# Seven half-size products for the down projection, earlier operand transfers for the SSD output product, and later squares in the attention norm

## The chip, the cores and the metric

The kernel runs on one core of a Trainium2 chip. A core has five engines with a queue each: TensorE (PE, with its weight loads shown as PEld), VectorE (DVE), ScalarE (ACT), GpSimd (POOL) and SyncE (SP), which here only issues transfers. The metric is the device time of one execution in microseconds; three runs are given and the median is compared.

## The reference

One decoder block over x (1024 tokens by 1024 channels, float32). What the change touches is, cut to the core:

```python
y = ssd_branch(...)                                # 1024 x 1024
merged = gate_ssd * (y_ssd @ w_ssd_o) + gate_att * (y_att @ w_attn_o)
o = rms_norm(o, subln_w, eps=SUBLN_EPS) * (1.0 - lam_init)   # per head of the differential attention
u = causal_dwconv(h2 @ w_up, conv_ffn_w, conv_ffn_b)         # 1024 x 5632
u_gate, u_val = jnp.split(u, 2, axis=-1)
f = (jax.nn.gelu(u_gate, approximate=True) * u_val) @ w_down # (1024 x 2816) @ (2816 x 1024)
x = x + g2 * rms_norm(f, post_norm2_w)
```

## The kernel before

All large products are float32 made of three passes: each operand is split into a high part `hi` (rounded to float32r) and a low part `lo = raw - hi`, and three matmuls add hi·hi, hi·lo and lo·hi into one PSUM bank. `split` (L80 to L82) makes the parts: ACT writes `hi` (L81), DVE writes `lo` (L82) from the raw tile and `hi`. Weights arrive by SP transfers into `wraw` (3 buffers) and are split into `whi` and `wlo` (4 buffers each). A matmul has a 128x128 stationary operand and a moving operand of up to 512 columns. Tiles that live longer come from 43 slots of 4 KB per partition (`Slots`), handed out in the order in which they were given back; a slot's new owner waits for the old one's last reader.

The stages in order of time are: the first norm and adaLN (0 to about 62 us of the span); the SSD's input product `xbc` with its convolution (L393 to L422), beside which DVE sums the rows of the adaLN weights (`ada_sum`, L364 to L370); the `z` product (L441 to L457); the chunked SSD scan; gates; q and k; the SSD output product `so` (L820 to L835); the differential attention (L851 to L1113); the attention output product `ao` (L1127 on); `w_out`, the second norm; the up projection `up` (L1294 to L1330); and the down projection, whose banks are called `fx` and `fy` (L1336 to L1390).

**Order of work.** A scheduler orders each engine's instructions before the run, by its own estimates of their durations and by when operands and buffers come free. Regions under `manual_schedule` keep the written order for the engines named: PE in `xbc`; PE, DVE and ACT in the attention. Nothing of `so`, `up` or `down` is written out by hand. An engine runs its queue in order; a waiting instruction holds all behind it. SP's queue issues every transfer of the kernel.

**`so`, L820 to L835.** For each of 8 blocks j: load the weight block (`load_block`), load the gate `gth` from DRAM (one buffer), 48 matmuls into a two-bank tile, two DVE instructions (L830) that multiply by the gate into `mout` (one buffer), store `mout` to `msd`. For j = 2 and 3 the first heads' q and k are loaded too.

**Attention.** Items (j, i) are head pair j and query block i. For each item: scores (PE), mask and maximum (DVE, L976 and L977 or L986 and L987), exponentials with row sums (ACT, L989, L997, L1000), reciprocal and combination into `p` (DVE, L1003 to L1005), transposes of `p` (PE, L1013), copies `aT` (ACT, L1014), product with v (PE, L1026). Between these, dense matmuls of later blocks are filled in (`fill`). After four items `norm_o` (L1030 to L1048) copies the four output blocks, and returns `squares` (four ACT instructions that square and sum, L1041); the next item's first turn runs them behind its scores and transposes and ahead of its exponentials. `first` and `second` (DVE, POOL and DVE again, L1035 to L1045) are background work behind.

**Up, L1294 to L1330.** The product h2 @ w_up is done by a scheme of seven half-size products in place of eight (with 2x2 blocks of both operands and sums of blocks, Strassen in Winograd's form). Per block pair `fb` (22 of them: gate block `fb`, value block `22 + fb`) there are 7 products of 12 matmuls each of 512 columns. `hl_tile` gives the split weights: 4 slots and the 8 `whi`/`wlo` buffers, 12 in turn. Bank `X` collects four products, `Y` two and `Z` one; between them ACT (L1305, L1313, L1315, L1321) and DVE (L1306, L1317, L1319) read the banks. Then the convolution (ACT L1325, DVE L1327), GELU (L1328), the gate product (DVE L1329) and the store of `g_` to DRAM (L1330).

**Down, L1336 to L1390.** For each half of the tokens the 22 blocks of `g_` are loaded (`gst`, 2 buffers of two blocks) and split into 22 slots; for each half of the channels 11 pairs of weight blocks are loaded and split, and 22 x 4 x 3 matmuls are added into 4 banks. That is 4 rounds of 264 matmuls. Each round ends with a sum of squares (ACT L1381) and a product (DVE L1382); the second round of a half also with the norm (DVE, POOL) and the store.

Of the kernel before, what the change touches and what calls it, by code (L numbers as in the profile page):

```python
# [17 lines left out]
P = 128  # L18
# [16 lines left out]
class Slots:  # L35
# [18 lines left out]
def kernel(ctx: ExitStack, tc: tile.TileContext, a: dict, out: bass.AP, dbg=None):  # L54
# [275 lines left out]
    gd = [dp.tile([P, S], F32, tag=f"gd{i}", name=f"gd{i}") for i in range(NFF)]  # L330
# [55 lines left out]
    brow = SL.get("brow")  # L386
    n_ada, rows_done = 0, 0
# [4 lines left out]
    with tc.manual_schedule(engines={EN.PE}):  # L392
        for b in range(12):  # L393
# [17 lines left out]
            xbcT.append(o)  # L411
            if b >= 2:
# [27 lines left out]
    n_ev = 0  # L440
# [17 lines left out]
    SL.put(*ev)  # L458
# [361 lines left out]
    gth = SL.get("gth")  # L820
    mout = SL.get("mout")
    for j in range(8):
        w = load_block(a["w_ssd_o"][j], f"wso{j}")
        ps = ps_mm(f"so{j}")
        SP.dma_start(gth, gsd[j])
        for half in range(2):
            block_half(ps[:, half, :], w, yT, half)
        for half in range(2):
            hsl = slice(half * HALF, (half + 1) * HALF)
            V.scalar_tensor_tensor(mout[:, hsl], gth[:, hsl], 1.0, ps[:, half, :], op0=ALU.add, op1=ALU.mult)  # L830
        SP.dma_start(msd[j], mout)
        if j in (2, 3):
            s = j - 2
            load_qk(s, qst[0][s], kst[0][s], klo[0][s])
    SL.put(gth, mout)  # L835
# [194 lines left out]
    def norm_o(j, grp):  # L1030
# [16 lines left out]
        bg.extendleft([(("norm", j, grp), second), (None, lambda: None), (None, lambda: None), (None, first)])  # L1047
        return squares  # L1048
# [14 lines left out]
    with tc.manual_schedule(engines={mybir.EngineType.PE, mybir.EngineType.DVE, mybir.EngineType.Activation}):  # L1063
# [5 lines left out]
        pend = squares = None  # L1069
        for t, (j, i) in enumerate(items):  # L1070
# [6 lines left out]
            def first_turn():  # L1077
                x[0] = transposes(t, 0)
                if squares is not None:
                    squares()  # L1080
# [5 lines left out]
            squares = None  # L1086
# [18 lines left out]
            if i % 4 == 3:  # L1105
                squares = norm_o(j, i // 4)
                pend = (j, i // 4)
            elif i % 4 == 2:
                pend = None
        squares()  # L1110
# [109 lines left out]
    hls = [SL.get(f"hls{i}") for i in range(4)]  # L1220
# [4 lines left out]
    def hl_tile(name):  # L1225
        nonlocal n_hl
        i = n_hl % 12
        n_hl += 1
        if i < 4:
# [27 lines left out]
    for fb in range(2):  # L1257
# [36 lines left out]
    for fb in range(NFF):  # L1294
        cg, cv = cgv[fb % 2]
        e1, e2 = evs[fb % 2][:, 0, :], evs[fb % 2][:, 1, :]
        if fb >= 2:
# [24 lines left out]
        g_ = ug[fb % 2]  # L1322
# [7 lines left out]
        SP.dma_start(gd[fb], g_)  # L1330
    SL.put(*sab, *hls, *cgv[0], *cgv[1], *evs)
    for n, _ in order:
        SL.put(*HB[n])
    SL.put(*ug, uv)

    g2r = SL.get("g2r")  # L1336
    SP.dma_start(g2r, rowd[3].broadcast_to([P, D]))
    fo = [SL.get(f"fo{i}") for i in range(4)]
    x1r = [SL.get(f"x1r{i}") for i in range(4)]
    tf = SL.get("tf", F32, (P, HALF))  # L1340
    gst = [SL.get(f"gst{i}", F32, (P, 2, HALF)) for i in range(2)]
    gT = None
    ssf = const("ssf", [P, 8, 2])
    rsf = const("rsf", [P, 8])
    for half in range(2):
        if half == 1:
            SL.put(*gT)
        gT = [None] * NFF
        for fb in range(NFF):
            gT[fb] = new_hl(f"g{half}_{fb}")  # L1350
            st = gst[fb // 2 % 2][:, fb % 2, :]
            SP.dma_start(st, gd[fb][:, half * HALF : (half + 1) * HALF])
            split(gT[fb][:, 0, :], gT[fb][:, 1, :], st)
        for ch in range(2):
            if ch == 0:
                acs = [ps_wa(f"fx{half}_0"), ps_wa(f"fx{half}_1"), ps_wb(f"fx{half}_2"), ps_wc(f"fx{half}_3")]
            else:
                mmx = [ps_mm(f"fy{half}_{i}") for i in range(2)]
                acs = [mmx[i // 2][:, i % 2, :] for i in range(4)]
            last = half == 1 and ch == 1  # L1360
            wd = {}
            sched = []
            for kp in range(NFF // 2):
                if not last or kp < NFF // 2 - 3:
                    sched += [(kp, q) for q in range(4)]
            if last:
                sched += [(kp, q) for q in range(4) for kp in range(NFF // 2 - 3, NFF // 2)]
            for kp, q in sched:
                if kp not in wd:
                    wd[kp] = load_moving(a["w_down"], 2 * kp, 2, ch * HALF, HALF, f"wd{half}_{ch}_{kp}")  # L1370
                tsl = slice(q * P, (q + 1) * P)
                for kk in range(2):
                    k = 2 * kp + kk
                    wh, wl = wd[kp][0][:, kk, :], wd[kp][1][:, kk, :]
                    T.matmul(acs[q], gT[k][:, 0, tsl], wh, start=(k == 0), stop=False)  # L1375
                    T.matmul(acs[q], gT[k][:, 0, tsl], wl, start=False, stop=False)  # L1376
                    T.matmul(acs[q], gT[k][:, 1, tsl], wh, start=False, stop=(k == NFF - 1))  # L1377
            csl = slice(ch * HALF, (ch + 1) * HALF)
            for q in range(4):
                i = 4 * half + q  # L1380
# [75 lines left out]
```

## Time and profile before

| | us |
|---|---|
| median of 3 runs (lowest, highest) | 1979.33 (1977.42, 1981.37) |
| profiled execution, whole | 1979.32 |
| its span, first to last instruction | 1977.5 |
| mean granted TensorE clock | 0.992 |

The views below give busy time by engine; a group's row has the line, the engine, the operation, output <- inputs and the shapes, then busy us and mean ns of one, then the engine's idle time just ahead of them and what ended it. Matmuls overlap, so the mean of one is longer than the distance between two. The stage times above are read from such windows.

### The profile page before, as it was taken

Reading aid. Unit: us, or ns where it says so; the run is one execution under the profiler, and the core shown is the slowest. Engines: PE = TensorE matmul, PEld = TensorE weight load, DVE = VectorE, ACT = ScalarE, POOL = GpSimd, SP = SyncE. Lnnn points to the kernel's source line nnn. Section 1 sums busy time; section 2 is a strip of 40 time slices with the busy share of each in tenths; the row PEclk is TensorE's granted clock in tenths of the full one; section 3 lists DMA queues with packets and bytes.
Section 4 is the critical chain, followed back from the end, with each engine's and each line's share of the span. In section 5 each row is a group of like instructions: output and inputs, shape, how many; then the busy total and the mean of one; then the engine's idle time right before and its main releaser. Section 6 shows DMA issues by size and latency. Waiting matters only on the chain.

```text
span 1977.5 us, 24442 instructions
## 1 busy us (share of the span) xinstructions
PE 1905.0 (96%) x9260; PEld 1579.5 (80%) x9260; DVE 1167.4 (59%) x1782; ACT 834.7 (42%) x1606; POOL 117.0 (6%) x114
## 2 busy tenths in 40 slices
PE   6999999999999999999999999979999999999997
PEld 4787998878888788888887887758888888788886
DVE  6967334565172247767666445599787777664322
ACT  5532225554232135655556322366454554543221
POOL 0000002542010000000000000000000000000000
PEclk9999999999999999999999999989999999999999
DMA  9834232235337636565623552212222222574531
GB/s 303 297 117 161 78 108 79 91 107 177 117 75 226 220 106 177 154 168 147 183 89 136 182 185 107 93 50 100 96 75 86 84 77 86 175 245 144 181 97 63
DMA packets 120414, 269.06 MB, mean 136 GB/s; under 512 B 13284, under 2 KB 44644, under 8 KB 120296
## 3 DMA queue, kind: packets, MB, share of 16 engines
q1 hardware_dynamic: 120296, 267.50, 42.5%
q8 instruction: 73, 1.20, 0.2%
q14 instruction: 45, 0.37, 0.1%
HBM read 201.37 MB, written 66.08 MB: 135 GB/s over the span
## 4 chain that ended last, share of the span: by engine, by line
PE 85%; DVE 5%; DMA 4%; ACT 3%; SPq 1%; issue 1%; POOL 0%; POOLq 0%; ACTq 0%; DVEq 0%
PE up L1247 5%; PE up L1248 5%; PE up L1249 5%; PE o L1026 3%; PE fy L1377 2%; PE fy L1376 2%; PE fy L1375 2%; PE fx L1377 2%; PE fx L1376 2%; PE fx L1375 2%; PE upy L1249 2%; PE upy L1247 2%; PE upy L1248 2%; PE xbc L103 2%; PE xbc L105 2%; PE xbc L104 2%
## 5 line engine op out<-in xcount | busy, mean ns | idle before, releaser
L1247 PE MATMUL up<-t,wu_t 128*128 128x512 f32 x264 | 107.1, 406 | 4.4 <-DVE cg L1306 3.5
L82 DVE TENSOR_TENSOR wd_lo<-wd_raw,wd_hi 128x1024 fp32r<-128x1024 f32 x44 | 53.8, 1225 | 96.6 <-ACT wd_hi L81 94.8
L1248 PE MATMUL up<-t,wu_t 128*128 128x512 f32 x264 | 104.0, 394 | 0.0
L1249 PE MATMUL up<-t,wu_t 128*128 128x512 f32 x264 | 103.4, 392 | 0.0
L1014 ACT COPY aT<-at 128x512 f32<-128x512 f32 (+2 forms) x96 | 45.9, 478 | 113.8 <-PE at L1013 113.8
L81 ACT ACTIVATE wd_hi<-wd_raw 128x1024 fp32r<-128x1024 f32 x44 | 46.6, 1059 | 96.8 <-PE fx L1377 52.9
L1026 PEld LDWEIGHTS o<-vt,aT 128*128 128x128 f32 x576 | 74.9, 191 | 10.1 <-ACT aT L1014 5.6
L1026 PE MATMUL o<-vt,aT 128*128 128x128 f32 x576 | 80.9, 277 | 1.3 <-ACT aT L1014 1.3
L81 ACT ACTIVATE wu_t<-sab 128x512 fp32r<-128x512 f32 x66 | 41.6, 632 | 79.2 <-PE up L1249 39.3
L1377 PE MATMUL fx<-wd_hi,g 128*128 128x512 f32 x176 | 68.7, 390 | 0.8 <-DVE g L82 0.7
L1247 PEld LDWEIGHTS up<-t,wu_t 128*128 128x128 f32 x264 | 49.9, 189 | 24.1 <-DVE cg L1306 9.3
L1249 PE MATMUL up<-b,wu_b 128*128 128x512 f32 x176 | 68.5, 389 | 0.0
L1376 PE MATMUL fx<-wd_lo,g 128*128 128x512 f32 x176 | 68.5, 389 | 0.0
L1375 PE MATMUL fx<-wd_hi,g 128*128 128x512 f32 x176 | 68.5, 389 | 0.0
L1248 PE MATMUL up<-b,wu_b 128*128 128x512 f32 x176 | 68.5, 389 | 0.0
L1375 PE MATMUL fy<-wd_hi,g 128*128 128x512 f32 x176 | 68.5, 389 | 0.0
L1376 PE MATMUL fy<-wd_lo,g 128*128 128x512 f32 x176 | 68.5, 389 | 0.0
L1377 PE MATMUL fy<-wd_hi,g 128*128 128x512 f32 x176 | 68.5, 389 | 0.0
L1247 PE MATMUL up<-b,wu_b 128*128 128x512 f32 x176 | 68.5, 389 | 0.0
L987 DVE TENSOR_REDUCE nmx<-sc 128x1 f32<-128x640 f32 (+3 forms) x64 | 65.6, 1024 | 2.1
L967 PE MATMUL sc<-kst,qst 128*128 128x512 f32 (+2 forms) x192 | 63.7, 340 | 0.0
L103 PE MATMUL xbc<-hT,wx_hi 128*128 128x512 f32 x160 | 63.6, 397 | 0.0
(381 smaller groups left out, 5588.5 us busy)
## 6 DMA issues: line engine op xcount, KB each, us to landing
wu_raw<-in_w_up SPq DMA_DIRECT2D x44, 512.0 KB, 3.5
wd_raw<-in_w_down SPq DMA_DIRECT2D x44, 512.0 KB, 3.7
adas<-in_w_ada SPq DMA_DIRECT2D x32, 512.0 KB, 5.7
gd<-ug SPq DMA_DIRECT2D x22, 512.0 KB, 2.7
gst<-gd SPq DMA_DIRECT2D x44, 256.0 KB, 3.5
adat<-in_w_ada SPq DMA_DIRECT2D x32, 256.0 KB, 5.9
qst<-qd SPq DMA_DIRECT2D x16, 512.0 KB, 5.0
kst<-khd SPq DMA_DIRECT2D x32, 256.0 KB, 4.9
```

The source lines that it names most:

```text
L81: A.activation(hi, raw, AF.Copy)
L82: V.tensor_tensor(lo, raw, hi.bitcast(F32), op=ALU.subtract)
L103: T.matmul(ps, lh, rh, start=(i == 0), stop=False)
L967: T.matmul(sc[:, n0:n1], qs_[s][:, tsl], ks_[s][:, n0:n1], start=True, stop=False)
L987: V.reduce_max(nmx[:, bq, s : s + 1], sc[:, :L], axis=AX.X, negate=True)
L1026: T.matmul(po_of[j, grp][:, qi, :], at[:, k, :], vt[j % 2][:, kt, :], start=(kt == 0), stop=(kt == i))
L1247: T.matmul(out_, wh, xh_, start=(k == 0 and not more), stop=False, skip_group_check=more)
L1248: T.matmul(out_, wh, xl_, start=False, stop=False, skip_group_check=more)
L1249: T.matmul(out_, wl, xh_, start=False, stop=(k == KH - 1), skip_group_check=more)
L1375: T.matmul(acs[q], gT[k][:, 0, tsl], wh, start=(k == 0), stop=False)
L1376: T.matmul(acs[q], gT[k][:, 0, tsl], wl, start=False, stop=False)
L1377: T.matmul(acs[q], gT[k][:, 1, tsl], wh, start=False, stop=(k == NFF - 1))
```

## The change

Three things are changed.

**Down.** It too becomes seven half-size products. The left operand is `g_` in 2x2 blocks (token half by half of the 22 channel blocks), the right one `w_down` in 2x2 blocks. The sums of left blocks s1 to s4 are made by POOL at the end of each pair of up blocks, and stored to DRAM with the blocks a11, a12, a22 (`gld`). For that the up blocks are run in the order 0, 11, 1, 12 and so on (`fbs`). The sums of right blocks t1 to t4 are made by POOL during the `xbc` and `z` stages (`down_sums`, 11 times; loads and stores too are issued by POOL) and kept in DRAM (`wtd`). Two slots fewer are left to `hl_tile`: it turns over 10 tiles instead of 12. In the down stage each product has 11 blocks in 6 pairs; the next product's left operand is loaded and split while one runs (`left_part(p + 1, kp)`).

**`so`.** Gate and output tile get two buffers each, weights are loaded two blocks ahead and gates one, and SP and PE keep the written order.

**Attention.** `squares` becomes the first of the background steps, so it is run behind the next item's exponentials; `first` comes behind that item's reciprocal, `second` later. At the end of the last head it is run when `out_o` needs it.

```diff
+    def get_last(self, *args):
+        self.free_list.insert(0, self.free_list.pop())
+        return self.get(*args)
...
+    wdr = [SL.get_last(f"wdr{i}", F32, (P, 2, HALF)) for i in range(2)]
+    wds = [SL.get_last(f"wds{i}", F32, (P, 2, HALF)) for i in range(2)]
+    def down_sums(k):
+        for i in range(2):
+            r0 = (k + KF * i) * P
+            G.dma_start(wdr[i].rearrange("p h c -> p (h c)"), a["w_down"][r0 : r0 + P, :])
+        (b11, b12), (b21, b22) = [(t[:, 0, :], t[:, 1, :]) for t in wdr]
+        t1, t2, t3, t4 = wds[0][:, 0, :], wds[0][:, 1, :], wds[1][:, 0, :], wds[1][:, 1, :]
+        G.tensor_tensor(t1, b12, b11, op=ALU.subtract)
+        G.tensor_tensor(t2, b22, t1, op=ALU.subtract)
+        G.tensor_tensor(t3, b22, b12, op=ALU.subtract)
+        G.tensor_tensor(t4, b21, t2, op=ALU.subtract)
+        for i in range(2):
+            G.dma_start(wtd[("12", "34")[i]][:, k, :, :], wds[i])
...
+            if b >= 2 and b % 2 == 0:
+                down_sums(b // 2 - 1)
...
+            if q == 0:
+                down_sums(n_dn)
+                n_dn += 1
...
-        w = load_block(a["w_ssd_o"][j], f"wso{j}")
-        ps = ps_mm(f"so{j}")
-        SP.dma_start(gth, gsd[j])
...
+    wso = [load_block(a["w_ssd_o"][j], f"wso{j}") for j in range(2)]
+    SP.dma_start(gths[0], gsd[0])
+    with tc.manual_schedule(engines={EN.SP, EN.PE}):
+        for j in range(8):
+            gth, mout = gths[j % 2], mouts[j % 2]
+            if j + 2 < 8:
+                wso.append(load_block(a["w_ssd_o"][j + 2], f"wso{j + 2}"))
+            if j + 1 < 8:
+                SP.dma_start(gths[(j + 1) % 2], gsd[j + 1])
...
+            if j in (2, 3):
+                s = j - 2
+                load_qk(s, qst[0][s], kst[0][s], klo[0][s])
+            SP.dma_start(msd[j], mout)
...
-        bg.extendleft([(("norm", j, grp), second), (None, lambda: None), (None, lambda: None), (None, first)])
-        return squares
+        bg.extendleft([(("norm", j, grp), second), (None, lambda: None), (None, first), (None, lambda: None), (None, squares)])
...
-    hls = [SL.get(f"hls{i}") for i in range(4)]
+    hls = [SL.get(f"hls{i}") for i in range(2)]
...
-        SP.dma_start(gd[fb], g_)
+        k = fb % KF
+        if fb < KF:
+            SP.dma_start(gld["a11"][:, k, :], g_[:, :HALF])
+            continue
+        SP.dma_start(gld["a12"][:, k, :], g_[:, :HALF])
+        SP.dma_start(gld["a22"][:, k, :], g_[:, HALF:])
+        (l11, l21), (l12, l22) = [(t[:, :HALF], t[:, HALF:]) for t in ug]
+        s1, s2, s3, s4 = gsum[0][:, 0, :], gsum[0][:, 1, :], gsum[1][:, 0, :], gsum[1][:, 1, :]
+        G.tensor_tensor(s1, l21, l22, op=ALU.add)
+        G.tensor_tensor(s2, s1, l11, op=ALU.subtract)
+        G.tensor_tensor(s3, l11, l21, op=ALU.subtract)
+        G.tensor_tensor(s4, l12, s2, op=ALU.subtract)
+        for n, t in (("s1", s1), ("s2", s2), ("s3", s3), ("s4", s4)):
+            SP.dma_start(gld[n][:, k, :], t)
...
+    downs = (("a11", "b11", bX), ("a12", "b21", bY), ("s2", "t2", bX), ("s1", "t1", bY), ("s3", "t3", bX), ("s4", "b22", bY), ("a22", "t4", bX))
...
+        SP.dma_start(st[:, :nk], gld[downs[p][0]][:, 2 * kp : 2 * kp + nk, :])
+        split(hi[:, :nk], lo[:, :nk], st[:, :nk])
...
+        for kp, q in sched:
+            if kp not in wd:
+                wd[kp] = right_part(p, kp)
+                left_part(p + 1, kp)
+            tsl = slice(q * P, (q + 1) * P)
+            gh, gl = gop[p % 2][kp]
+            for kk in range(min(2, KF - 2 * kp)):
+                k = 2 * kp + kk
+                wh, wl = wd[kp][0][:, kk, :], wd[kp][1][:, kk, :]
+                T.matmul(bank[q], gh[:, kk, tsl], wh, start=(k == 0 and not more), stop=False, skip_group_check=more)
+                T.matmul(bank[q], gh[:, kk, tsl], wl, start=False, stop=False, skip_group_check=more)
+                T.matmul(bank[q], gl[:, kk, tsl], wh, start=False, stop=(k == KF - 1), skip_group_check=more)
```

Left out above: after each product four banks are read, by ACT into `es` or by DVE with `es` added, and each finished 128x512 piece is squared and summed (ACT) and multiplied by `g2r` (DVE); a token block's norm, residual sum and store follow its second piece, four of them in the product before the last and four behind the last.

More of the change, by code (lines that the diff above doesn't have):

```diff
@@ L1332 @@
+        G.tensor_tensor(s1, l21, l22, op=ALU.add)
[4 more added lines that the diff above has]
+            SP.dma_start(gld[n][:, k, :], t)
     for n, _ in order:
         SL.put(*HB[n])
-    SL.put(*ug, uv)
+    SL.put(*sab, *hls, *cgv[0], *cgv[1], *evs, *ug, uv, *gsum)
+    KP = (KF + 1) // 2
+    gst = [SL.get(f"gst{i}", F32, (P, 2, HALF)) for i in range(2)]
```

176 lines of the change are left out of this document (95 added, 81 removed).

## Prediction

> **What bounds the kernel now.** I read the page first, then windows by stage, then groups of instructions that keep shapes apart, the transfers, and the timeline at the places that the change touches.
>
> ```profile
> span 1977.5 us, 24442 instructions
> PE 1905.0 (96%) x9260; PEld 1579.5 (80%) x9260; DVE 1167.4 (59%) x1782; ACT 834.7 (42%) x1606; POOL 117.0 (6%) x114
> ...
> PE 85%; DVE 5%; DMA 4%; ACT 3%; SPq 1%; issue 1%; POOL 0%; POOLq 0%; ACTq 0%; DVEq 0%
> ```
>
> TensorE is busy in 96% of the span and holds 85% of the chain that ended last. A matmul taken away there is worth its pace, unless something else comes to feed TensorE too slowly. So the questions are the pace, and who feeds. The windows below have the length, then PE, PEld, DVE, ACT and POOL busy with counts, the granted clock, the DMA share and GB/s.
>
> ```profile
> 80.00:102.00 22.00, 22.00 (x99) 18.21 (x98) 18.75 (x17) 9.65 (x11) 0.00 (x0) 1.00 0.88 302
> 102.00:124.00 22.00, 22.00 (x99) 18.22 (x98) 10.20 (x9) 6.44 (x6) 0.00 (x0) 1.00 0.25 93
> ...
> 146.00:168.00 22.00, 22.00 (x95) 17.53 (x94) 19.79 (x18) 4.91 (x6) 0.00 (x0) 1.00 0.77 267
> ...
> 1400.00:1500.00 100.00, 100.00 (x437) 80.92 (x437) 77.00 (x100) 49.73 (x74) 0.00 (x0) 1.00 0.24 79
> 1740.00:1800.00 60.00, 60.00 (x267) 49.67 (x266) 30.58 (x37) 26.57 (x40) 0.00 (x0) 1.00 0.63 208
> 1735.00:1967.00 232.00, 232.00 (x1024) 192.07 (x1024) 91.10 (x108) 69.80 (x99) 4.22 (x6) 1.00 0.43 146
> ```
>
> In `xbc` (first three), `up` (fourth) and `down` (last two) TensorE never rests, at a granted clock of 1.00. The down stage runs 1024 matmuls in 232 us: 0.2266 us each.
>
> **A. Seven products for eight in `down`.**
>
> ```profile
> L1375 PE MATMUL fx<-wd_hi,g 128*128 128x512 f32 x176 | 68.5, 389 | 0.0
> ...
> L1375 PE MATMUL fy<-wd_hi,g 128*128 128x512 f32 x176 | 68.5, 389 | 0.0
> ...
> L82 DVE TENSOR_TENSOR wd_lo<-wd_raw,wd_hi 128x1024 fp32r<-128x1024 f32 x44 | 53.8, 1225 | 96.6 <-ACT wd_hi L81 94.8
> ...
> L81 ACT ACTIVATE wd_hi<-wd_raw 128x1024 fp32r<-128x1024 f32 x44 | 46.6, 1059 | 96.8 <-PE fx L1377 52.9
> ...
> wd_raw<-in_w_down SPq DMA_DIRECT2D x44, 512.0 KB, 3.7
> ...
> gst<-gd SPq DMA_DIRECT2D x44, 256.0 KB, 3.5
> ```
>
> Before: 3 lines x 176 x 2 banks' names = 1056 matmuls (the 389 ns is one matmul's latency; they overlap). After: 7 products x 11 blocks x 4 token blocks x 3 = 924, of the same shape. 132 fewer x 0.2266 = **-29.9 us**.
>
> Can the stage be fed? A pair of blocks is now 24 matmuls, 24 x 0.2266 = 5.44 us, and needs one right and one left operand: ACT 2 x 1.059 = 2.1 us, DVE 2 x 1.225 = 2.45 us, and two transfers of 512 KB, 1.05 MB in 5.44 us = 193 GB/s. The window 1740:1800 moved 208 GB/s with TensorE busy in all 60 us. A left buffer's turn is landing 3.5 + 1.06 + 1.23 = 5.8 us; two buffers give one each 2.9 us, below 5.44. The added bank reads (about 0.69 us on DVE or 0.6 on ACT, four a product) are covered by the next product, which uses the other four banks, and DVE stays under 27 of 30 us even in the busiest product. The tail behind the last matmul keeps its shape. So I count A in full.
>
> **F. The turn from `up` to `down`.** The first product needs only a11, finished one up block earlier; but the slots of its left parts come free while the last block's products run, and a left part that waits for a store (SP is in order) holds right parts behind it. Before, the same turn had its loads tangled too. Bounds 0 to +8 (one store 2.7, POOL sums 4 x 1.04, one load 3.5, less the cover of about 2 us); I take **+1.5**, since the product that needs the late blocks comes 30 us after.
>
> **B. `so` in written order.**
>
> ```profile
> L105 PE MATMUL so<-yT,wso_lo 128*128 128x512 f32 x128 | 50.9, 399 | 2.4 <-DVE wso_lo L82 2.4
> ...
> L103 PE MATMUL so<-yT,wso_hi 128*128 128x512 f32 x128 | 50.8, 398 | 1.0 <-DVE mout L830 1.0
> ...
> ACT wso_hi L81 <- DMA wso_raw<-in_w_ssd_o: 36.9, 5, 16.1
> ...
> w_q_raw<-in_w_q SPq DMA_DIRECT2D x8, 512.0 KB, 4.6
> ```
>
> TensorE waited 2.4 us for split weights, which waited for late loads, and 1.0 us for `mout`. With loads two blocks ahead (a block is 48 x 0.2266 = 10.9 us) and two buffers both go: -3.4. Against it, the store of block j, which waits for its DVE reads, now stands in SP ahead of the weights of j+3; these are needed 22 us later, so that wait is covered. If the attention's first weight load is put behind the last store, TensorE waits for it and its split, up to 4.6 + 1.06 + 1.23 = +7. Bounds -3.4 to +3.6; I take **-3.0**.
>
> **C. Squares behind the exponentials.** The timeline at the turn of a head:
>
> ```profile
> 808.99 0.31 ACT L1041 ACTIVATE osb<-osb 128x128 f32<-128x128 f32 x1
> ...
> 809.13 0.69 DVE L977 TENSOR_REDUCE nmx<-sc 128x2 f32<-128x512 f32 x1
> ...
> 810.17 0.46 ACT L1000 ACTIVATE p<-sc,nmx 128x256 f32<-128x256 f32 x1
> ...
> 812.20 0.44 PE L1013 MATMUL at<-ident,p 128*128 128x128 f32 x2 [1.15 <-DVE p L1005]
> ...
> L1013 PE MATMUL at<-ident,p 128*128 128x128 f32 x288 | 48.1, 276 | 11.0 <-DVE p L1005 10.8
> ```
>
> The squares start at 808.99 and the exponentials at 810.17, so they look worth 1.2 us. But the maximum, without which no exponential starts, ends only at 809.82: what they really delay is 0.35 us. TensorE's waits for `p` are 10.8 us in the whole attention. Bounds 0 to -10.8; 7 turns of a head x 0.3 = **-2.1**. The squares now stand on ACT ahead of the next `aT` copy, which has the fill matmuls as cover. DVE's `first` no longer stands ahead of the reciprocal.
>
> **D. The end of the attention.** With no next item the squares are now issued only when the output block is wanted, behind 16 fill steps.
>
> ```profile
> 1086.05 0.30 ACT L1041 ACTIVATE osb<-osb 128x128 f32<-128x128 f32 x1
> ...
> 1087.80 1.01 POOL L130 TENSOR_TENSOR sqt<-sqt,nhalf 128x4 f32<-128x4 f32 x1 [29.36 <-DVE sqt L129]
> ...
> 1089.53 0.68 DVE L1045 TENSOR_TENSOR osb<-osb,sqt 128x512 f32<-128x512 f32 x1
> ```
>
> From the first square to the end of the norm is 1090.2 - 1086.05 = 4.2 us, until now under the fill. Bounds 0 to +4.2; `ao` products can be put into part of it: **+1.0**.
>
> **E. POOL's sums.** 11 x 4 in `xbc` and `z`, 11 x 4 in `up`: 88 instructions of 128x512, and POOL is idle there (0.00 in the windows above), so its own queue is no issue until the scan's first POOL work, behind at most one last round (0 to +3). The price is what they do to DVE.
>
> ```profile
> L805 DVE TENSOR_TENSOR sw<-sw,rops 128x1024 f32<-128x1024 f32 x4 | 12.1, 3018 | 0.0
> ...
> L1329 DVE TENSOR_TENSOR ug<-ug,uv 128x1024 f32<-128x1024 f32 x22 | 26.8, 1219 | 0.0
> ...
> L804 POOL TENSOR_TENSOR qf<-qf,ropc 128x1024 f32<-128x1024 f32 x4 | 9.6, 2393 | 93.2 <-DVE sw L803 93.2
> 322.16 1.04 POOL L615 TENSOR_TENSOR xdd<-xd,sm 128x512 f32<-128x512 f32 x1 [0.63 <-DVE xd L613]
> ...
> 1505.81 0.69 DVE L82 TENSOR_TENSOR wu_b<-wu_raw,wu_b 128x512 fp32r<-128x512 f32 x1 [1.87 <-ACT wu_b L81]
> ...
> 1508.39 0.69 DVE L1317 TENSOR_TENSOR cv<-up,evs 128x512 f32<-128x512 f32 x1 [1.89 <-PE up L1249]
> ...
> 1509.78 0.19 PEld L1247 LDWEIGHTS up<-t,wu_t 128*128 128x128 f32 x1
> ...
> adas<-in_w_ada SPq DMA_DIRECT2D x32, 512.0 KB, 5.7
> ```
>
> A DVE product that meets POOL's (L805 beside L804) takes 3018 ns where its like (L1329) takes 1219: it stands still while POOL works. A POOL sum of 128x512 is 1.04 us, so four hold DVE's two-operand work for up to 4.2 us. All 88 would be 92 us.
>
> [...]
>
> In `up`: a pair of blocks is 168 matmuls, 38 us; DVE has 23% of it free, 8.7 us, more than 4.2. The tightest point is the read of bank X (L1317), behind which the last product loads at 1509.78. DVE was idle for 1.87 and 1.89 us on the way, 3.8 in all, so 4.2 us of lock make the read 0.4 late, against 1509.78 - (1508.39 + 0.69) = 0.7 us of room. Bounds 0 to 11 x 1 = +11; I take **+1.5**. Ten weight tiles in place of twelve cost nothing: the splits may still run ten products of 12 x 0.2266 = 2.7 us ahead, 27 us, which 4.2 us of lock do not use up.
>
> In `xbc`: a round is two loads (5.7 us), four sums (4.2) and a store (2.7), 12.6 us, so 1.75 rounds or 7.3 us of lock in 22. DVE's spare time is 3.3, 11.8 and 2.2 us in the three windows: it falls 4 to 5 us behind in the full ones and catches up in the others. TensorE has one block of room (10.9 us) less the convolution (about 5 us), just enough. Bounds 0 to +10; I take **+1.5**.
>
> [...]
>
> **The sum.** -29.9 + 1.5 - 3.0 - 2.1 + 1.0 + 1.5 + 1.5 = -29.5. The profiled execution took 1979.32 us, 1.8 around the span of 1977.5, and is the median of the runs to 0.01. Forecast: 1979.3 - 29.5 = **1950**.
>
> **Rivals.**
>
> 1. *The lock decides* (slower). POOL's sums hold DVE where TensorE waits for DVE: `xbc` (19.8 of 22 us busy) and bank X in `up`. Price up to 92 us; from a third of it exposed (31 of 92) the gain is gone; at half, 1979.3 - 31 + 46 = 1994. For it: the 3018 ns. Against it: 23% of DVE free in `up`, 3.8 us of idle ahead of the tight read. 9%. At just a third exposed it ends as no change: 4%.
> 2. *The feed of `down` is late at the turns*: SP holds right parts behind left parts that wait for stores, at the first product (+8) and for the POOL sums, and B turns into +3.6. 1950 + 6.5 + 6.6 = 1963. For it: one queue for all. Against it: 30 us between a block's end and its use. 17%.
> 3. *More comes free in the attention*: two thirds of the 10.8 us of waits for `p` go, as the background order eases DVE too: 1950 - 5 and no cost in D and E (-4) = 1941. Against it: the maximum at 809.82 is not moved. 8%.
> 4. The forecast, 1944 to 1957: 62%.
>
> **Numbers.** Two runs of this kernel can be told apart from about 0.2%, 4 us. Faster: 62 + 17 + 8 = 87%; same 4%; slower 9%. With every favourable bound the sum is 1935, with every unfavourable one 1989; the range 1942 to 1968 leaves out most of rivals 1 and the ends, under 2 in 10.
>
> **What would show it.** Right: 924 `down` matmuls at 0.2266 us with TensorE busy throughout; no wait for `wso_lo` or `mout`; exponentials directly behind the maximum; DVE products next to POOL sums near 1.7 us instead of 0.69, without TensorE waits. Wrong: TensorE waiting for DVE `cu`, `cg` or `cv`; idle time ahead of `down`'s matmuls released by transfers; a wait ahead of the attention's first fill.

## The result, and the profile after

| | before | after |
|---|---|---|
| median, us (runs: lowest, highest) | 1979.47 (4: 1977.42, 1981.37) | 1953.73 (4: 1947.88, 1956.52) |
| profiled execution, us | 1979.32 | 1951.79 |
| its span, us | 1977.5 | 1950.0 |
| mean granted TensorE clock | 0.992 | 0.987 |

The ratio is 0.9866, interval 0.984 to 0.9893: 25.7 us faster by the medians, 27.5 by the two spans. The forecast was 1950. The sum was near; several of its terms were not, as the next table shows. It is read from the start of the first or last matmul of a stage in the two timelines.

| stretch | before, us | after, us | difference | prediction |
|---|---|---|---|---|
| start to last `xbc` matmul | 202.16 | 214.22 | +12.06 | E: +1.5 |
| from there to first `so` matmul | 404.74 | 404.50 | -0.24 | 0 |
| `so`, to the first scores | 106.71 | 103.73 | -2.98 | B: -3.0 |
| scores, first to last | 354.13 | 347.87 | -6.26 | C: -2.1 |
| to the last `ao` matmul | 116.02 | 116.39 | +0.37 | D: +1.0 |
| to the first `up` matmul | 94.32 | 94.17 | -0.15 | 0 |
| to the last transpose `h2tr` | 22.73 | 24.24 | +1.51 | not named |
| to the last `up` matmul | 426.04 | 427.55 | +1.51 | E: +1.5 |
| to the last `down` matmul | 240.13 | 209.51 | -30.62 | A and F: -28.4 |
| to the end | 10.53 | 7.85 | -2.68 | 0 |

The page of the kernel after, its span, busy times, the TensorE clock in 40 slices, and two groups:

```profile
span 1950.0 us, 24628 instructions
...
PE 1875.2 (96%) x9128; PEld 1556.3 (80%) x9128; DVE 1236.1 (63%) x1790; ACT 845.9 (43%) x1614; POOL 275.9 (14%) x246
...
PEclk8998999999999999999999999989999999999999
...
L1279 PE MATMUL up<-t,wu_t 128*128 128x512 f32 x264 | 107.0, 405 | 4.7 <-DVE cg L1340 4.6
...
L107 PE MATMUL xbc<-hT,wx_hi 128*128 128x512 f32 x160 | 64.6, 404 | 9.1 <-DVE cu L433 9.0
```

PE has 9128 matmuls instead of 9260, the 132 of term A, and POOL is busy for 159 us more. The fourth digit of the clock row is lower than before (so is the first, ahead of `xbc`), and new are 9.0 us in which `xbc` waited for `cu`, the convolution's instructions on VectorE. The windows of the kernel after, with the columns of the prediction's windows:

```profile
80.00:102.00 22.00, 22.00 (x98) 18.21 (x97) 19.51 (x15) 9.35 (x10) 11.83 (x11) 1.00 0.91 343
...
146.00:168.00 22.00, 22.00 (x95) 17.53 (x94) 19.63 (x17) 6.05 (x6) 13.81 (x12) 1.00 0.97 346
1400.00:1500.00 100.00, 99.97 (x434) 80.47 (x433) 84.64 (x98) 49.32 (x73) 12.95 (x9) 1.00 0.29 98
1740.00:1800.00 60.00, 60.00 (x266) 49.73 (x265) 37.23 (x35) 28.48 (x35) 6.51 (x3) 1.00 0.82 283
1735.00:1940.00 205.00, 205.00 (x906) 169.81 (x905) 116.88 (x127) 89.03 (x122) 12.61 (x9) 1.00 0.64 213
```

In `down` (last two) TensorE never rests, at 205 / 906 = 0.2263 us a matmul, although 283 GB/s are moved where 208 were. In `xbc` the DMA share at 146 to 168 rose from 0.77 to 0.97. Groups of the whole kernel after, with shapes kept apart:

```profile
L1455 PE MATMUL dx<-wdt_hi,g_hi 128*128 128x512 f32 x132 | 51.3, 389 | 0.0
...
L107 PE MATMUL so<-yT,wso_hi 128*128 128x512 f32 x128 | 50.2, 392 | 2.1 <-DVE mout L867 1.5 <-ACT yT L809 0.7
...
L1050 PE MATMUL at<-ident,p 128*128 128x128 f32 x288 | 47.9, 275 | 8.0 <-DVE p L1042 8.0
```

In `so` the waits for `wso_lo` (2.4 us before) are gone, but the one for `mout` is not: 1.5 us, 1.0 before. In the attention the waits for `p` fell from 10.8 to 8.0 us.

**Where `xbc` lost 12 us.** VectorE's timeline of the kernel before (start, length, instruction, idle time ahead of it and what ended it):

```profile
162.96 5.25 DVE L370 SCALAR_TENSOR_TENSOR accr<-adas,scl,accr 128x1024 f32<-128x1024 f32 x4
170.24 1.28 DVE L370 SCALAR_TENSOR_TENSOR accr<-adas,scl,accr 128x1024 f32<-128x1024 f32 x1 [2.04 <-DMA adas<-in_w_ada]
...
172.58 1.28 DVE L408 SCALAR_TENSOR_TENSOR cu<-xbc,vec,cu 128x1023 f32<-128x1023 f32 x1
```

and at the same place of the kernel after:

```profile
166.07 1.79 DVE L376 TENSOR_SCALAR accr<-adas,scl 128x1024 f32<-128x1024 f32 x1
167.89 6.15 DVE L378 SCALAR_TENSOR_TENSOR accr<-adas,scl,accr 128x1024 f32<-128x1024 f32 x4
177.42 1.28 DVE L378 SCALAR_TENSOR_TENSOR accr<-adas,scl,accr 128x1024 f32<-128x1024 f32 x1 [3.37 <-DMA adas<-in_w_ada]
178.62 1.22 DVE L86 TENSOR_TENSOR wgs_lo<-wgs_raw,wgs_hi 128x1024 fp32r<-128x1024 f32 x1
179.75 1.27 DVE L433 SCALAR_TENSOR_TENSOR cu<-xbc,vec,cu 128x1023 f32<-128x1023 f32 x1
182.29 1.28 DVE L378 SCALAR_TENSOR_TENSOR accr<-adas,scl,accr 128x1024 f32<-128x1024 f32 x1 [1.27 <-DMA adas<-in_w_ada]
183.50 1.27 DVE L433 SCALAR_TENSOR_TENSOR cu<-xbc,vec,cu 128x1022 f32<-128x1022 f32 x1
```

TensorE's timeline of the same kernel at that place:

```profile
179.93 0.39 PE L109 MATMUL xbc<-hT,wx_lo 128*128 128x512 f32 x1
188.35 0.77 PE L107 MATMUL xbc<-hT,wx_hi 128*128 128x512 f32 x1 [8.03 <-DVE cu L433]
188.91 0.63 PE L108 MATMUL xbc<-hT,wx_hi 128*128 128x512 f32 x1
189.34 0.63 PE L109 MATMUL xbc<-hT,wx_lo 128*128 128x512 f32 x1
```

The three `cu` instructions read the bank that the next block needs, and in VectorE's queue they stand behind and between the sums `accr` of the adaLN rows. Those wait for `adas` (3.37 and 1.27 us here) and run beside POOL's sums (6.15 us for four that took 5.25 before). The order itself is not new: from 66 us to the end of `xbc` VectorE's queue holds the same 91 instructions in the same order before and after, with one memset (`acT`) more. TensorE stood still: from the start of one matmul to that of the next it was 8.4 us. Behind the wait two matmuls are 0.43 us apart instead of 0.2266. The windows of the kernel after show how long:

```profile
184.00:190.00 6.00, 1.65 (x4) 1.39 (x5) 5.11 (x4) 1.71 (x3) 6.00 (x7) 0.50 0.13 53
190.00:196.00 6.00, 6.00 (x20) 4.69 (x20) 4.73 (x4) 1.96 (x3) 0.26 (x1) 0.70 0.99 334
196.00:202.00 6.00, 6.00 (x28) 4.99 (x27) 0.00 (x0) 0.43 (x2) 5.55 (x5) 1.00 0.07 24
```

The granted clock is 0.50, then 0.70, then 1.00. The twelve matmuls from 188.35 on took 5.2 us where 2.7 are the pace: 2.5 us more. With 1.1 us lost at 109.5, 8.2 + 2.5 + 1.1 = 11.8 of the 12.06 us are found.

### The profile page after: what moved, and what is told of

It is laid out like the page before. It is cut to its first block, busy times and chain, and to the rows that moved or that the text cites. A ratio compares the mean times of both kernels' runs of the same rounds, so it can differ in the third digit from the quotient of the medians.

```text
span 1950.0 us, 24628 instructions
## 1 busy us (share of the span) xinstructions
PE 1875.2 (96%) x9128; PEld 1556.3 (80%) x9128; DVE 1236.1 (63%) x1790; ACT 845.9 (43%) x1614; POOL 275.9 (14%) x246
## 3 DMA queue, kind: packets, MB, share of 16 engines
q8 instruction: 72, 1.18, 0.3%
## 5 line engine op out<-in xcount | busy, mean ns | idle before, releaser
L86 DVE TENSOR_TENSOR g_lo<-gst,g_hi 128x1024 fp32r<-128x1024 f32 (+1 forms) x42 | 49.3, 1181 | 55.9 <-ACT g_hi L85 54.6
L134 POOL TENSOR_TENSOR sqt<-sqt,nhalf 128x4 f32<-128x4 f32 x16 | 16.1, 1007 | 478.2 <-DVE sqt L133 478.2
L85 ACT ACTIVATE g_hi<-gst 128x1024 fp32r<-128x1024 f32 (+1 forms) x42 | 41.2, 989 | 74.9 <-DMA gst<-gld_s 31.2
L107 PE MATMUL xbc<-hT,wx_hi 128*128 128x512 f32 x160 | 64.6, 404 | 9.1 <-DVE cu L433 9.0
L1361 DVE SCALAR_TENSOR_TENSOR ug<-cg,vec,ug 128x1023 f32<-128x1023 f32 (+1 forms) x44 | 56.5, 1283 | 14.1 <-ACT ug L1359 13.4
L109 PE MATMUL xbc<-hT,wx_lo 128*128 128x512 f32 x160 | 63.2, 395 | 0.0
L108 PE MATMUL xbc<-hT,wx_hi 128*128 128x512 f32 x160 | 63.2, 395 | 0.0
L1005 PE MATMUL sc<-klo,qst 128*128 128x512 f32 (+2 forms) x192 | 63.2, 345 | 0.0
L107 PE MATMUL z<-wz_hi,hT 128*128 128x346 f32 (+1 forms) x192 | 61.8, 323 | 0.1
L108 PE MATMUL z<-wz_lo,hT 128*128 128x346 f32 (+1 forms) x192 | 61.8, 322 | 0.0
```

Of the source, the lines that this page charges most:

```text
L107: T.matmul(ps, lh, rh, start=(i == 0), stop=False)
L108: T.matmul(ps, lh, rl, start=False, stop=False)
L109: T.matmul(ps, ll, rh, start=False, stop=(i == n - 1))
```

## The experiments

The line numbers in a run's rows are those of its own kernel. Where a run has one execution only, its stretches are compared.

**Transfers or subtractions.** Two halves of `down_sums`, each by itself. The transfers alone, `xfer_only`:

```diff
-        G.tensor_tensor(t1, b12, b11, op=ALU.subtract)
...
-        G.tensor_tensor(t4, b21, t2, op=ALU.subtract)
-            G.dma_start(wtd[("12", "34")[i]][:, k, :, :], wds[i])
+            G.dma_start(wtd[("12", "34")[i]][:, k, :, :], wdr[i])
```

> Transfers of the down sums without the sums: the raw weight blocks are loaded and stored by POOL, the four subtractions are left out, so the down product gets raw blocks in place of t1 to t4. If late adaLN transfers hold VectorE (theory of the transfers), TensorE still waits 5 to 9 us for cu and the last xbc matmul is at 209 to 216. If POOL's lock on VectorE holds it, it is at 202 to 204, with accr at 1.28 us. If only both together exceed VectorE's room, it is at 202 to 207 here and in the run without transfers.

The subtractions alone, `sums_only`:

```diff
-        for i in range(2):
+        for i in range(2 if k == 0 else 0):
             r0 = (k + KF * i) * P
...
-        G.tensor_tensor(t1, b12, b11, op=ALU.subtract)
+        G.tensor_tensor(t1, b12, xbcT[k + 1][:, :HALF], op=ALU.subtract)
...
-        for i in range(2):
-            G.dma_start(wtd[("12", "34")[i]][:, k, :, :], wds[i])
+        for i in range(2 if k == KF - 1 else 0):
+            for m in range(KF):
+                G.dma_start(wtd[("12", "34")[i]][:, m, :, :], wds[i])
```

> The sums of the down weights without their transfers in xbc: the raw blocks are loaded once, the first subtraction of round k reads the convolved block k+1 so that the rounds are spread over xbc (about one in 10.9 us, denser than the one in 16 us of the change), and the stores all stand behind the last round; t1 to t4 hold other numbers. Theory of the transfers: last xbc matmul at 202 to 204, no wait for cu over 1 us, though accr takes 1.5 us. Theory of the lock: 209 to 216. Both needed: 202 to 207.

The last `xbc` matmul was at 206.98 with the transfers alone (+4.8 against before) and at 205.98 with the subtractions alone (+3.8). VectorE's groups in `xbc` (62 to 206 us), first of the kernel before:

```profile
L370 DVE SCALAR_TENSOR_TENSOR accr<-adas,scl,accr 128x1024 f32<-128x1024 f32 x27 | 34.6, 1281 | 3.1 <-DMA adas<-in_w_ada 2.6
```

the same view of the kernel after:

```profile
L378 DVE SCALAR_TENSOR_TENSOR accr<-adas,scl,accr 128x1024 f32<-128x1024 f32 x27 | 40.5, 1500 | 10.2 <-DMA adas<-in_w_ada 9.8
L86 DVE TENSOR_TENSOR wx_lo<-wx_raw,wx_hi 128x1024 fp32r<-128x1024 f32 x10 | 15.9, 1610 | 14.2 <-ACT wx_hi L85 14.2
L433 DVE SCALAR_TENSOR_TENSOR cu<-xbc,vec,cu 128x1022 f32<-128x1022 f32 x11 | 14.0, 1276 | 0.1
```

of `xfer_only`:

```profile
L378 DVE SCALAR_TENSOR_TENSOR accr<-adas,scl,accr 128x1024 f32<-128x1024 f32 x27 | 34.6, 1282 | 11.7 <-DMA adas<-in_w_ada 11.4
```

and of `sums_only`:

```profile
L378 DVE SCALAR_TENSOR_TENSOR accr<-adas,scl,accr 128x1024 f32<-128x1024 f32 x27 | 45.8, 1696 | 2.4 <-DMA adas<-in_w_ada 1.9
```

The two causes are cleanly apart in the last columns: transfers make the sums wait (11.4 us against 2.6) and leave their length; subtractions make them longer (1696 ns against 1281) and leave the waits. Neither theory alone holds, and the third (each within VectorE's room, only both beyond it) is nearest, though each half already cost 4 to 5 us, and after the wait of `xfer_only` the clock was at 0.50 for 3.4 us as well. Both halves ran denser here than in the change, so the two numbers are not shares of the 12. The convolution itself (`cu`) is not lengthened by POOL at all: 1276 ns, 1278 before.

**VectorE's queue** (`no_accr`). All rounds kept, but the last seven of the eight sums of the fourth adaLN row left out: those that stand ahead of and between the `cu` above.

```diff
-        else:
+        elif r < 3:
             V.scalar_tensor_tensor(acc, adas[u % 4], scl[:, k : k + 1], acc, op0=ALU.mult, op1=ALU.add)
```

> The changed kernel with all its rounds in place, but VectorE's last seven of eight sums of the fourth adaLN row (accr, L378) left out; that row then holds one eighth of its sum. If TensorE's wait near 180 comes from VectorE's queue, in which the convolution cu stands behind sums that wait for adas and run beside POOL, the wait is gone (under 1 us) and the last xbc matmul is at 203 to 206, though POOL's transfers and subtractions are all there. If the transfers or subtractions hold the convolution itself (its operands, ACT, the bank), the wait stays at 5 us or more and the last matmul at 209 or later.

The last `xbc` matmul was at 202.53 and the wait near 180 was gone. The windows of this run:

```profile
146.00:168.00 22.00, 22.00 (x95) 17.53 (x94) 19.66 (x16) 5.13 (x5) 14.17 (x12) 1.00 0.98 355
168.00:190.00 22.00, 22.00 (x99) 18.22 (x98) 11.66 (x9) 6.16 (x6) 9.14 (x12) 1.00 0.79 277
```

POOL (14.2 and 9.1 us busy) and the transfers (shares of 0.98 and 0.79) work about as in the change, and TensorE does not wait. So the transfers and the lock reach TensorE's path by way of these sums: they make them late, and they stand in front of the convolution in one queue. The run's 1944.65 us is a time without that work, so it is no version to keep. It takes the sums away altogether; that moving the last adaLN row's sums behind the convolution, or into `z`, would be enough is likely by the timeline, but was not tried.

**Other places for the rounds.** First, in `moved`, four calls in `z` and seven behind the scan.

```diff
-            if b >= 2 and b % 2 == 0:
-                down_sums(b // 2 - 1)
...
+            if q == 0 and n_dn < 4:
                 down_sums(n_dn)
...
         for half in range(2):
             gate_out(ps[:, half, :], half, gsd[j])
+        for _ in range(2 if j > 3 else 1):
+            if n_dn < KF:
+                down_sums(n_dn)
+                n_dn += 1
```

> All eleven rounds of POOL's down sums are taken out of xbc: four go into z and seven behind the last gate blocks of the scan (sections gs and q/k), where VectorE is 37 to 42 per cent busy. If the rounds are what cost xbc its 12 us (last xbc matmul at 214.2 instead of 202.2), that matmul is back at 202 to 203, the 8.4 us wait of TensorE for cu is gone and the whole is 1938 to 1943 us. If the 12 us come from something else that the change did to xbc (another order of VectorE's queue, other slots), it stays at 208 or later and the whole at 1948 to 1954. If the new places cost as much, xbc is back but z, gs or q/k are 5 us or more longer.

1969.07 us, ratio 0.9953 [0.994, 0.9967]: slower than the change, by the third case of the expectation. The four calls in `z` needed slots that were free from the start, and POOL ran them in `xbc`; it ended at 203.24, so four rounds there cost only 1.1 us. But the stretch from the last `gs` matmul to `so` grew from 69.15 to 90.70. VectorE's timeline of this run:

```profile
556.07 0.74 DVE L814 SCALAR_TENSOR_TENSOR yT<-ytr,vec,yT 128x512 fp32r<-128x512 f32 x1
581.63 2.27 DVE L841 TENSOR_TENSOR qf<-qf,sw 128x1024 f32<-128x1024 f32 x1 [24.82 <-POOL qf L839]
```

POOL's one instruction of the rotation stood behind two more rounds in POOL's queue, VectorE waited 24.8 us for it, and TensorE 17 us behind that. As in `xbc`, an instruction that TensorE needs stood in one queue behind work that it does not need; here the queue is POOL's.

Then, in `spread`, four in `xbc` as in the change, five in `z` in slots that come free late, two beside the gates:

```diff
+    wdr = [SL.get_last(f"wdrz{i}", F32, (P, 2, HALF)) for i in range(2)]
...
+            if q == 0 and n_dn < 9:
...
+        if n_dn < KF:
+            down_sums(n_dn)
+            n_dn += 1
```

and in `spread_end` the same, with the end of the attention in smaller steps:

```diff
-        fill(16)
+        run_bg(1)
+        fill(2)
+        run_bg(2)
+        fill(4)
+        run_bg(2)
+        fill(10)
         out_o(*pend)
```

> All three edits, with the eleven rounds of down sums placed anew: four in xbc as the first four of the change, five in z in slots that only come free behind xbc, two beside the gate blocks ahead of the rotation of q and k (L835). If the 12 us of xbc come from rounds too many there, its last matmul is at 203 to 204, z stays at 92.2 us, the stretch from the last gs matmul to so at 69.2 us (90.7 in the run that held the rotation up), and the whole is 1940 to 1944 us. If late rounds of z hold the scan's POOL work, the scan is longer by 5 to 10 us and the whole 1946 to 1952.

> As the run before, and the last squares, the rest of the norm's first half and its second half are run in three steps between the last fill matmuls in place of all behind them. If the 2.4 us wait of ao for the last output block is the norm's chain started too late, it falls under 1 us, and the stretch from the last scores to the last ao matmul from 116.4 to 114.5 to 115.5 us. If something else holds it there (the copies of the last probabilities, ACT), it stays at 116 to 117.

`spread` took 1951.44 us (0.9873 [0.9855, 0.9892]), no better than the change: `xbc` ended at 202.65, as expected, but `z` was 8.4 us longer, which neither case had foreseen. (In `spread_end`, with the same four rounds, `xbc` ended at 205.23.) ScalarE's timeline in `z` of this run:

```profile
253.60 0.78 ACT L85 ACTIVATE wz_hi<-wz_raw 128x692 fp32r<-128x692 f32 x1 [4.54 <-DMA wz_raw<-in_w_zdt]
```

A weight load that SP issues just before it is needed (its median from issue to landing is 3.2 us) met two of POOL's loads and took 8.6. `spread_end` took 1947.72 us (0.9838 [0.9824, 0.9852]); the stretch from the last scores to the last `ao` matmul was 114.28 us against 115.77 in `spread`, and TensorE's 2.0 us wait there for the last output block is gone, so the norm's chain was indeed started too late. In this profile, of the slowest of its five runs, the next stretch gave that back: to the first `up` matmul it took 96.43 us against 94.37. There a wait of 2.0 us for split weights of `w_out`, near 1190, was followed by 3.4 us at a granted clock of 0.50; in `spread` one of 1.5 us was not.

The third placing has five in `xbc`, two early in `z`, four beside the gates, and the end of `spread_end`; the change itself ran beside it.

> All three edits, the three steps at the end of the attention, and a third placing of the eleven rounds: five in xbc, two at the start of z (so that none of POOL's loads meets the weight loads of z near 245), four beside the gate blocks behind the scan. If the stalls come from POOL's loads that meet a late SP load and from rounds behind the fifth in xbc, xbc ends at 202 to 205, z is 92.2 long again, scores-to-ao stays near 114.5, and the whole is 1938 to 1943 us. If every place costs about as much, the sum from the start to the first so matmul stays 9 us or more above the 606.9 of before, and the whole is at 1946 to 1952.

> The changed kernel itself once more, beside the run before it on the same chip: 1948 to 1956 us. Its own runs lay 8.6 us apart where those of before lay 4. If the wait in xbc is a meeting of transfers that falls out differently from run to run, the profiled run's wait for cu is another than 8.4 us; if it is fixed by VectorE's order, it is 8 to 9 us again.

`spread2`: 1947.46 us (0.9838 [0.9821, 0.9855]), its five runs all under the four of the change beside them, 1952.66 us (0.9869 [0.985, 0.9888]). By the medians it beats both kernels, the change by 5 us, though the two intervals touch; yet it misses its forecast: the first `so` matmul came at 615.35, 8.5 us behind before. `xbc` ended at 206.33, `z` was 1.0 longer, the scan 3.3. So its second case is the nearer: `spread`, `spread_end` and `spread2` pay 8.8, 10.3 and 8.5 us ahead of `so`, where the change pays 11.8 and, in its second profile, 10.0. In the change's own second profile the wait for `cu` was 6.5 us, not 8.4, and `xbc` ended at 212.37; in `up_no_sums` below, whose `xbc` is that of the change, at 213.94. The place of the wait is the same each time; its length differs, which fits transfers that fall out differently, and a stage's 2 to 3 us in one profile should not be read closer.

**The squares alone** (`squares_alone`). The edit also moves `first` and `second` later on VectorE, as the change does.

```diff
-        bg.extendleft([(("norm", j, grp), second), (None, lambda: None), (None, lambda: None), (None, first)])
-        return squares
+        bg.extendleft([(("norm", j, grp), second), (None, lambda: None), (None, first), (None, lambda: None), (None, squares)])
```

> The kernel before with only the squares moved. If they delayed the exponentials at all 15 turns of a group (by 0.3 us at a turn of a head, by 1.2 us at a turn inside a head, where the first maximum is done early), the stretch of the scores falls from 354.1 to about 348 and the whole by 5 to 6.5 us. By the prediction's count, 7 turns of 0.3, it falls to 352 and the whole by 2. The stretch behind it, to the last ao matmul, is 0.3 to 1 us longer in both.

Scores 348.08 us, and 117.73 behind them (+1.7): 1974.07 us, ratio 0.9971 [0.9958, 0.9983], 4.4 us. The stretch of the scores is what the first theory foretold; the whole is not (5 to 6.5 us), because of the stretch behind. There a wait of 2.2 us for the last output block, near 1091, was followed by 3.4 us at a granted clock of 0.50, 1.7 us lost; in the change a wait of 2.0 us at the same place was not. ScalarE's timeline of the kernel before at a turn inside a head:

```profile
873.37 0.58 ACT L1014 COPY aT<-at 128x512 f32<-128x512 f32 x1 [2.69 <-PE at L1013]
873.85 0.32 ACT L1041 ACTIVATE osb<-osb 128x128 f32<-128x128 f32 x1
...
875.03 0.89 ACT L989 ACTIVATE p<-sc,nmx 128x768 f32<-128x768 f32 x1
...
876.38 0.27 ACT L1014 COPY aT<-at 128x128 f32<-128x128 f32 x1
```

and of the kernel after:

```profile
879.64 0.59 ACT L1051 COPY aT<-at 128x512 f32<-128x512 f32 x1 [2.67 <-PE at L1050]
880.12 0.91 ACT L1026 ACTIVATE p<-sc,nmx 128x768 f32<-128x768 f32 x1
...
881.49 0.28 ACT L1051 COPY aT<-at 128x128 f32<-128x128 f32 x1
```

From the first copy to the second it was 3.01 us and is 1.85. Here the exponentials were delayed by all four squares, 1.18 us, and so was the copy for which TensorE waited at 876: its matmul started 0.72 us behind the one ahead of it, 0.24 us in the kernel after. The prediction had looked at a turn between heads only.

But not all turns inside a head are like this one. TensorE's order of matmuls is the same before and in this run, so the starts of the same matmuls can be compared turn by turn. Of the 6.05 us the seven turns between heads gave 3.7, 0.53 each; the eight inside a head gave 2.3, 0.6 at two of them (this is one) and 0 to 0.5 at the others. So the first theory has the right sum with the wrong parts. At a turn between heads the first wait for `p` fell by 0.3 us (1.15 to 0.85 at 812 before and 819 after), as the prediction worked out; most of the rest comes at the next block of transposes. There VectorE's mask and maximum of the next item stand behind the short `first` instead of `second`: in the kernel before the mask starts 0.72 us behind the end of `p`, here 0.50. That is VectorE's part of the edit; no run takes it apart from the squares.

**`so` alone** (`so_alone`): the lines L820 to L835 of before replaced by those of the change.

> The kernel before with only the written order and the second buffers of so. By the prediction the stretch from the first to the last so matmul falls from 97.0 to 94.0 us and nothing else moves, the whole by 3 us. By the rival the load of the attention's first weights, put behind the last store, gives it back: the turn from the last so matmul to the first scores is longer than 9.75 us by up to 7.

First to last `so` matmul 93.96 us (96.97 before), 9.75 to the scores as before: 1976.04 us, 0.9983 [0.9973, 0.9994], 2.8 us. The size is as predicted, and the rival's +3.6 did not come. The parts are not: the waits for `wso_lo` are gone, but the one for `mout` is 1.5 us, as in the change, and two for `yT`, 0.95 together, are new. What makes up for them is the clock. In the kernel before, the wait of 2.06 us for `wso_lo` was followed by 3.4 us at a granted clock of 0.50, 1.7 us lost. In `tail_banks` below, whose `so` is that of before, a wait of 2.05 us at the same place was not, and its `so` took 95.42 us; against that, the edit is worth 1.5 us.

**`up` without POOL's sums** (`up_no_sums`).

```diff
-        G.tensor_tensor(s1, l21, l22, op=ALU.add)
...
-        G.tensor_tensor(s4, l12, s2, op=ALU.subtract)
-        for n, t in (("s1", s1), ("s2", s2), ("s3", s3), ("s4", s4)):
+        for n, t in (("s1", l21), ("s2", l22), ("s3", l11), ("s4", l12)):
```

> The sums s1 to s4 in up are left out and the raw quarters are stored in their place. If POOL's lock costs up its 2 to 3 us, the 1.8 us wait of TensorE for cg near 1351 goes and the stretch from the first up matmul to the last of down is 659 us instead of 661.3. If the wait belongs to the start of the stage (weights late), it stays within 0.5 us and the stretch at 661; VectorE's 128x512 products fall to 0.69 us either way.

From `h2tr` to the last `up` matmul 426.05 us, against 427.55 in the change and 428.54 in its second profile: the sums cost 1.5 to 2.5 us. (The kernel before has 426.04, but with the first three `down` matmuls, 0.7 us, among them.) The wait near 1351 went too. The stretch to `h2tr` stayed at 24.22, so its 1.5 us have another cause. VectorE's timelines show one that no run tests: ahead of the first subtraction that `h2tr` needs (`hraw`) it now runs three sums of `up`'s weights and three splits, two and two before. VectorE's groups in `up` of the kernel after show whom the lock meets:

```profile
L86 DVE TENSOR_TENSOR wu_t<-sab,wu_t 128x512 fp32r<-128x512 f32 x63 | 56.2, 894 | 1.6 <-ACT wu_t L85 1.6
L1344 DVE TENSOR_TENSOR sab<-wu_raw 128x512 f32<-128x512 f32 x42 | 45.4, 1117 | 1.9 <-DMA wu_raw<-in_w_up 1.9
...
L1351 DVE TENSOR_TENSOR cv<-up,evs 128x512 f32<-128x512 f32 x22 | 15.1, 687 | 8.2 <-PE up L1281 7.5
```

Without the sums the first two take 685 and 689 ns. The reads of a bank (`cv`, 687) are untouched.

**The tail** (`tail_banks`). The kernel before with the banks of its rounds exchanged.

```diff
-            if ch == 0:
+            if ch == 1:
                 acs = [ps_wa(f"fx{half}_0"), ps_wa(f"fx{half}_1"), ps_wb(f"fx{half}_2"), ps_wc(f"fx{half}_3")]
```

> The kernel before with the banks of the down rounds exchanged, so that the last round has four tiles of one bank each instead of two tiles of two. If the two-bank tile is what makes the last but one piece wait for the last matmul, the time from the last matmul's start to the end falls from 10.5 to 7.8 us, and only the last piece is finished behind it. If the shorter tail of the change comes from its other order of work, it stays at 10.5. The turn from up to down may be longer by 1 to 6 us, since the first round then waits for banks of up.

7.68 us from the last matmul to the end, 10.53 before: the two-bank tile is what made the tail longer. ScalarE's last squares in the kernel before:

```profile
1960.70 0.60 ACT L1381 ACTIVATE tf<-fy 128x512 f32<-128x512 f32 x1 [0.76 <-DVE fo L1382]
...
1967.47 0.60 ACT L1381 ACTIVATE tf<-fy 128x512 f32<-128x512 f32 x1 [6.09 <-PE fy L1377]
...
1968.92 0.60 ACT L1381 ACTIVATE tf<-fy 128x512 f32<-128x512 f32 x1 [0.76 <-DVE fo L1382]
```

and in the kernel after:

```profile
1939.26 0.60 ACT L1427 ACTIVATE es<-dx 128x512 f32<-128x512 f32 x1 [2.71 <-PE dx L1457]
...
1942.66 0.60 ACT L1427 ACTIVATE es<-dx 128x512 f32<-128x512 f32 x1 [2.71 <-PE dx L1457]
```

Before, the pieces 3 and 4 shared one two-bank tile, and both waited for its last matmul; in the change each has a tile, and one piece is left behind the end.

## Why the prediction was right, and where only its sum was

**A** was right to the tenth: 924 matmuls, no wait among them, 209.51 us for 924 x 0.2266 = 209.4 (1.0 us more in the second profile, 0.5 of it one wait for a weight block). **F** cost nothing: the first `down` matmul starts 0.23 us behind the last of `up`, and the turn before had lost 1.5 us to waits; A and F together gave 30.6, not 28.4. **B** was right in size and place, -3.0, but partly by luck: of its two waits one went, the other stayed, and the clock gave the 1.7 us that the prediction did not have.

**C** had the right mechanism and a term too small: -6.3 against -2.1. Both its factors were short, by the turns of `squares_alone`: a turn between heads gave 0.53 us, not the 0.3 of its first wait, and the eight turns inside a head, 2.3 us together, were left out. Rival 3 had about this size, and its reason, that the background's order eases VectorE too, fits what the prediction missed between heads; it is argued from the timeline and not tested apart. **D** was +0.4, not +1.0: TensorE waits 2.0 us for the last output block, as foretold, but less than before for the copies ahead of it (1.8 us, 2.7 and 0.7 before). The +1.7 in the squares alone is mostly the clock.

**E** is where the step failed. In `up` it was right: 1.5 to 2.5 us. In `xbc` it was +12.06 (10.2 and 11.8 in two more profiles), beyond even the bound of 10. The prediction set VectorE's room against the lock alone, and found "one block of room (10.9 us) less the convolution". The lock's size was not what failed: a round took about 16.7 us, not 12.6, and its four sums 5.9, not 4.2, so that 22 us held 7.8 us of sums for the 7.3 forecast. (The 1.04 us is one row of a group, `xdd`, whose mean was 1392 ns in the kernel before.) Three things were missing. POOL's loads slow the loads of `adas` (5.7 us to landing before, 6.5 after, 7.5 in `xfer_only`, 5.2 in `sums_only`), so VectorE's sums wait 9.8 us, not 2.6; `xfer_only` prices that at +4.8 by itself. The convolution stands behind those sums in one queue, so their waits are its own; without them `xbc` ended at 202.53. And this wait was paid again by the clock, 2.5 us.

That VectorE stands still beside POOL is seen in the trace of before: at the first of the four places L804 ran on POOL from 552.52 to 554.91, L805 on VectorE from 552.97 to 555.99, 1.08 us past POOL's end and near the 1.22 of its like. In `xbc` `accr` (1281 to 1500 ns) and `wx_lo` (1223 to 1610), whose inputs all lie in SBUF, were lengthened; `cu` (1278 to 1276), which reads a bank in PSUM, was not. That did not keep TensorE's path free, since `cu` stands in one queue with sums that were lengthened.

Rival 1 saw the right place (`cu` in `xbc`), and the warning "TensorE waiting for DVE `cu`" came true; but 12 + 1.5 us is far from the third of 92 from which it decides. Rival 2 did not come about. That the total fell within 4 us is luck: three errors nearly cancel, +10.6 in `xbc`, -4.2 in the attention, -2.7 in the tail, which the prediction had said "keeps its shape" without looking at which tiles its banks share.

## What to carry to other kernels

Price helper work on an idle engine not by its own length but by the queues that it reaches: find what it delays (here sums that wait for a load), and then what stands behind that in the same queue. In-order queues turned a few late transfers and longer sums into an 8 us wait of TensorE in `xbc`, by way of VectorE, and two rounds of sums into one of 17 us in `moved`, by way of POOL. A gain or loss of 1 to 2 us in one profile can be the clock's (1.7 us behind the 2.06 us wait in `so` of before): look at the granted clock behind each wait before it is put down to the edit. When a gain is read off one turn of a loop, look at each kind of turn that the loop has.

## What the runs showed of the hardware

After the 8.4 us wait TensorE's granted clock was 0.50, and matmuls started 0.427 us apart for 5.2 us. After 3.7 us in `xfer_only` it was 0.92 over the 22 us from 168 on; after 2.8 us in `sums_only` and 1.5 us in `moved` it was 1.00 from 168 to 190. A shorter wait was followed by the half pace too, but not each time: at one place of `so` a wait of 2.06 us was followed by 3.4 us at 0.50 in the kernel before and again in `squares_alone`, and one of 2.05 us in `tail_banks` was not. What decides it no run shows.

A VectorE TENSOR_SCALAR with one SBUF tensor (`accr`, first of a row) was lengthened in `xbc` as well: 747 ns before, 1093 after, by the means of three each.

POOL's loads of 512 KB took a median of 7.7 us from issue to landing; those of the same matrix issued by SP in `down` took 4.4, at another time and load. POOL's stores of 512 KB (`wtd`) took 5.1. The prediction's round had 5.7 for its loads and 2.7 for the store, the medians of `adas` and `gd`, both issued by SP in the kernel before.
